# A two-layer retention/latent-attention trunk: one more eviction buffer, a second norm bank, and sums and transfers placed one step ahead

## The chip, the cores and the metric

The kernel runs on one core of a Trainium2 chip. The metric is the device time of one execution in microseconds (us), the median over several runs. A core has a matrix engine (TensorE, PE in the profile), a vector engine (VectorE, DVE), an activation engine (ScalarE, ACT), GpSimd (POOL) and a queue engine (SyncE, SP) that issues most of the transfers. Each engine works through its own list of instructions in order and waits on semaphores for the others. TensorE reads its operands from the on-chip memory (SBUF) and writes sums into PSUM banks of 512 fp32 columns; another engine has to evict a bank before it is used again.

## The reference

One sequence of 512 tokens passes two layers of width 2048; everything is float32. Each layer first normalises its input and modulates it by a conditioning vector c; the branch's output is gated by c too, and added to x.

```python
c_act = jax.nn.silu(c)
for i in range(DEPTH):
    mod = (c_act @ ada_w[i] + ada_b[i])[:, None, :]
    shift, scale, gate = jnp.split(mod, 3, axis=-1)
    h = rmsnorm(x, norm_g[i]) * (1.0 + scale) + shift
    j = i // N_MIXERS
    if i % N_MIXERS == 0:
        y = retention_branch(h, positions, ret_w_in[j], ret_gn_g[j], ret_w_out[j])
    else:
        y = mla_branch(h, positions, mla_w_in[j], ...)
    x = x + gate * y
return rmsnorm(x, final_norm_g)
```

Layer 0 is retention with 8 heads. `h @ w_in` gives q and k (256 columns a head), v and a gate g (512 a head). q and k are rotated by the position, the scores q k^T are multiplied by a decay that falls with the distance of the tokens, and score times v is normalised per head, multiplied by silu(g) and projected back by `w_out`. Layer 1 is latent attention with 16 heads. `h @ w_in` gives two latents of 512 columns (for q and for k, v), a rotary key of 64 columns and a gate of 2048 columns, on which silu is taken; the latents are normalised and projected up to q, k and v, then softmax attention, times the gate, and the output projection.

## The kernel before, in words

Float32 products run as products of two rounded parts: a tile is split into a high part (a cast, on ACT, `split` at L135) and a low part (the difference, on DVE, L136), and each product is three matmuls, high x high, low x high and high x low (L161 to L163, L809 to L811, L1390). Nearly every weight tile therefore passes SP (load), ACT (cast) and DVE (difference) before TensorE can use it. Some products save matmuls by a seven-product scheme (`seven_steps`): it needs sums of the four quarter blocks of the activations (`form_sums`, L447) and combined weights.

The work is a list of steps. A step holds the matmuls of a few weight tiles (a step of a gate block is 24 matmuls of 128x512), and a list "beside" of loads, forming work (ACT, DVE) and extra products that are issued with it. The steps' loads and splits are issued ahead of their products by a fixed number of steps. What a step carries beside is written out by hand; a layer that records the instructions orders those of a step on each engine, and its pools give buffers in rotation, so that a tile waits for the last reader of the one whose buffer it gets.

Three regions matter here, in order of time.

*Retention (about 900 to 1440 us).* `retention(h, ...)` (L1161 on) makes a head out of 14 pieces, and `place` puts piece i beside step first + i. The heads lie at `n_p + 16*(h//2) + 4*(h%2)`: two heads overlap, and four such pairs follow each other. The first pair stands beside the last projection steps, the other three beside the output projection of earlier heads (`o1_product`, L1390, with weights o_r loaded at L1376 and split into o_whi and o_wlo) and beside the modulation sums of the layers to come (`mod`, loaded at L1087 on SP, two buffers, summed on DVE at L1092). The pieces that load are `load_qk(0)` and `load_qk(1)` (two transfers of 256 KB each, tile name qk_r, from DRAM where the projection put q and k; four buffers "ld"), `load_decay` (256 KB, one buffer "dec"), `load_v` (four transfers) and `load_gates` (four). All are on SP's queue with the weight and modulation loads. `rope(n, j)` (DVE, L1156 to L1158, then a split) rotates them, `scores` and `values` multiply on TensorE, `decay_scores` (L1206) applies the decay.

*The front of layer 1 (about 1440 to 1472 us).* The last retention output, the sum of squares, the factors of the norm and the first products of layer 1 overlap, with the tokens in two halves of 256. `norm_sums`, `norm_factors` and `norm_spread` (L1484 to L1494) turn a half's sums of squares into a row of factors that is spread over all partitions by four small matmuls (x_r, L1138) into a PSUM bank `norm2["r"]`, its left columns for half 0, its right for half 1. `h2_pair` (L1499) multiplies x by the factors out of that bank (h2f, DVE, L1505), adds the shift on ACT (the high part, L1512) and forms the low part on DVE (L1517). `ga_half` (L1642) are the products of gate block 0 by a half.

*Gate blocks 0 and 1 (about 1472 to 1550 us) and the latents (from 1550 us).* `g2_steps(gi)` (L1627) makes the eight steps of a gate block: four PSUM banks of 512 columns. At the end `evac` takes silu of each bank on ACT (sgs, L1630) into a buffer of the rotation "sg" (three buffers) and GpSimd stores it to DRAM (sg_d, L1632). `ga` is block 0 and `g1` block 1, `ga[7]` and `g1[7]` their last steps. Beside eight of these steps stands `form_sums` (L1731), which forms the sums for the latents' seven products: two additions (L450), four on half tiles (L452 to L455), then casts and differences; the products themselves (xc, sc, zc, yc, L809 to L811) follow block 1. Beside the last step of block 0 and the first of block 1 the rotary key (kr) is formed on ACT and DVE.

Of the kernel before, what the change touches and what calls it, by code (L numbers as in the profile page):

```python
# [49 lines left out]
def hybrid_trunk_kernel(  # L50
# [44 lines left out]
    def big(name, dt=F32R):  # L95
        return base.tile([P, 2, T], dt, tag="big", bufs=16, name=name)
# [7 lines left out]
    def tmp(name, shape=(P, T)):  # L104
        return base.tile(list(shape), F32, tag="tmp", bufs=6, name=name)
# [4 lines left out]
    def aux(name):  # L110
        return psum.tile([P, T], F32, tag="aux", bufs=4, name=name)
# [41 lines left out]
    def rows(w, u, n, c0, cn):  # L153
        return w[u * n * P : (u + 1) * n * P, c0 : c0 + cn].rearrange("(k p) n -> p k n", p=P)
# [46 lines left out]
    def w_block(w, ki, b):  # L201
        return w[0][:, ki, b * P : (b + 1) * P], w[1][:, ki, b * P : (b + 1) * P]
# [4 lines left out]
    def act_row(t):  # L207
        return t[:, 0, :], t[:, 1, :]
# [13 lines left out]
    a_col = [base.tile([P, KD], F32, name=f"a_col{i}") for i in range(2)]  # L222
# [224 lines left out]
    def form_sums(u, acts, sums, staged, more, late=False, apart=False):  # L447
        e, o = (tmp(f"h_{2 * u + i}_f") for i in range(2))
        for f, kt in ((e, 2 * u), (o, 2 * u + 1)):
            DVE.tensor_add(f, acts[kt][:, 0, :].bitcast(F32), acts[kt][:, 1, :].bitcast(F32))  # L450
        f = staged(f"sums_{u}_f")
        DVE.tensor_add(f[0][:, 0, :], e[:, H:], o[:, H:])  # L452
        DVE.tensor_sub(f[0][:, 1, :], f[0][:, 0, :], e[:, :H])
        DVE.tensor_sub(f[1][:, 0, :], e[:, :H], e[:, H:])
        DVE.tensor_sub(f[1][:, 1, :], o[:, :H], f[0][:, 1, :])  # L455

        def part():
            for i in range(2):
                s = sums[2 * u + i] = sums_tile(u + 8 * i if apart else 2 * u + i, more)
                split(f[i], s[:, :, 0, :], s[:, :, 1, :])  # L460

        if late:
            return part
        part()
# [78 lines left out]
    for t in range(NT):  # L543
        queued(square, t)
        queued(silu, t)
        if t == 0:
            queued(
                lambda: DVE.scalar_tensor_tensor(
                    out=bias1, in0=bias_c[0][:, KD:], scalar=1.0, in1=norm_c[0], op0=ALU.add, op1=ALU.mult
# [191 lines left out]
    def plain_steps(nu, kn, parts, cn, name, take, n, lhs, rhs, evac, seeded=False, **kw):  # L741

        banks = {}

        def step(u):
            w = {}

            def load():
                w["raw"] = base.tile([P, kn, cn], F32, tag="raw", bufs=3, name=f"{name}_{u}_r")
                for dst, src in parts(u):  # L750
                    nc.sync.dma_start(dst(w["raw"]), src)

            def prepare():
                w["hl"] = [
                    base.tile([P, kn, cn], F32R, tag=tag, bufs=3, name=f"{name}_{u}_{tag[1]}") for tag in ("whi", "wlo")
                ]
                split(w["raw"], *w["hl"])

            def multiply():
                if u == 0:  # L760
                    for b in range(n):
                        banks[b] = take(f"{name}_{b}")
                order = [(ki, b) for ki in range(kn) for b in range(n)]
                if u in (0, nu - 1):
                    order = [(ki, b) for b in range(n) for ki in range(kn)]
                for ki, b in order:
                    last = u == nu - 1 and ki == kn - 1
                    kt = u * kn + ki
                    mm3(banks[b], lhs(w["hl"], ki, kt, b), rhs(w["hl"], ki, kt, b), kt == 0, last, seeded)

            def follow():
                if u == nu - 1:
                    for b in range(n):
                        evac(b, banks[b])

            res = Step(load, prepare, multiply, follow, **{k: v(u) for k, v in kw.items()})
            res.w, res.banks = w, banks
            return res

        return [step(u) for u in range(nu)]  # L780
# [354 lines left out]
    def spread(ps, diag, n0, n):  # L1135

        for t in range(n):
            PE.matmul(ps[:, (n0 + t) * P : (n0 + t + 1) * P], ones, diag[:, t * P : (t + 1) * P], start=True, stop=True)  # L1138
# [14 lines left out]
    def rope_half(b1, b2, second, dst, name):  # L1153
        cos, sin = rotary
        t1, t2 = (tmp(f"{name}_t{i}") for i in range(2))
        DVE.tensor_mul(t1, b1, sin if second else cos)  # L1156
        DVE.tensor_mul(t2, b2, cos if second else sin)
        (DVE.tensor_add if second else DVE.tensor_sub)(t1, t1, t2)  # L1158
        split(t1, dst[:, 0, :], dst[:, 1, :])

    def retention(h, own, own2=None):  # L1161


        raws, sg, qk, v, s_hl, aside, ys, yn = {}, [], [], [], [], {}, [], []

        def fetch(key, tag, src_d, r0):
            raws[key] = l1_tile(tag, 4, f"{key}_{h}_r")
            nc.sync.dma_start(raws[key], src_d[r0 : r0 + P, :])

        def load_qk(n):  # L1170
            for j in range(2):
                fetch(f"qk{n}{j}", "ld", qk_d, (4 * h + 2 * n + j) * P)
# [14 lines left out]
        def rope(n, j):  # L1187
            dst = (own2 or own)(f"qk_{h}_{n}_{j}p")
            rope_half(raws[f"qk{n}0"], raws[f"qk{n}1"], j == 1, dst, f"rope_{h}_{n}_{j}")
            qk.append(dst)  # L1190
# [70 lines left out]
        def form_input():  # L1261
# [18 lines left out]
        return [  # L1280
            {"load": lambda: load_qk(0)},
            {"form": lambda: rope(0, 0)},
            {"form": lambda: rope(0, 1)},
            {"load": lambda: load_qk(1)},
            {"form": lambda: rope(1, 0)},
            {"form": lambda: rope(1, 1)},
            {"multiply": scores},
            {"load": load_decay},
            {"load": load_v, "form": decay_scores},
            {"load": load_gates, "form": split_v, "multiply": values},  # L1290
            {"form": group_norm},
# [25 lines left out]
    n_p = len(steps)  # L1317
    steps += block
    heads = [retention(0, k4), retention(1, k4, odd)]


    x1 = []
# [109 lines left out]
    for n in range(3):  # L1432
        block = []
        cols = range(4) if n % 2 == 0 else range(3, -1, -1)
# [35 lines left out]
    for u in range(4):  # L1470
        step = Step()
# [10 lines left out]
    norm2 = {}  # L1482
# [7 lines left out]
        norm2["diag"] = token_factors(norm2["s"], 2 * half, 2, f"x1_{half}")  # L1490

    def norm_spread(half):
        if half == 0:
            norm2["r"] = aux("x1_r")  # L1494
        spread(norm2["r"], norm2["diag"], 2 * half, 2)

    h2 = [None] * KD

    def h2_pair(u, half):  # L1499

        cols = slice(half * H, (half + 1) * H)
        sides = []
        for kt in (2 * u, 2 * u + 1):
            t = tmp(f"h2f_{half}_{kt}")[:, :H]
            DVE.scalar_tensor_tensor(  # L1505
                out=t, in0=x1[u][:, kt % 2, cols], scalar=a_col[1][:, kt : kt + 1], in1=norm2["r"][:, cols],
                op0=ALU.mult, op1=ALU.mult,
            )
            if h2[kt] is None:
                h2[kt] = big(f"h2_{kt}")  # L1510
            hi, lo = (h2[kt][:, a, cols] for a in range(2))
            ACT.activation(hi, t, AF.Identity, bias=b_col[1][:, kt : kt + 1])  # L1512
            sides.append((kt, t, hi, lo))

        def lows():
            for kt, t, hi, lo in sides:
                DVE.scalar_tensor_tensor(  # L1517
                    out=lo, in0=t, scalar=b_col[1][:, kt : kt + 1], in1=hi.bitcast(F32), op0=ALU.add, op1=ALU.subtract
                )

        return lows

    def h2_pairs(*which):

        late = None
        for u, half in which:
            lows = h2_pair(u, half)
            if late is not None:
                late()
            late = lows  # L1530
        late()
# [45 lines left out]
    for i, (multiply, follow) in enumerate(  # L1577
# [5 lines left out]
        step = Step(multiply=multiply, follow=follow)  # L1583
# [40 lines left out]
    def l2_tile(tag, bufs, name, shape=(P, T), dt=F32):  # L1624
        return pools["l2"].tile(list(shape), dt, tag=tag, bufs=bufs, name=name)

    def g2_steps(gi, **kw):  # L1627
        def evac(b, ps):
            sgs = l2_tile("sg", 3, f"sgs_{gi}_{b}")
            ACT.activation(sgs, ps, AF.Silu)  # L1630
            r0 = (gi * 4 + b) * P
            POOL.dma_start(sg2_d[r0 : r0 + P, :], sgs)  # L1632

        return plain_steps(
            8, 2, lambda u: [(whole, rows(w_mla_in, u, 2, 1088 + gi * 512, 512))], 512, f"g2_{gi}", acc, 4,
            lambda w, ki, kt, b: w_block(w, ki, b), lambda w, ki, kt, b: act_row(h2[kt]), evac, **kw,
        )


    ga = g2_steps(0, seeded=True)  # L1640
# [79 lines left out]
    g1 = g2_steps(1)  # L1720
# [7 lines left out]
    def more2(shape, name):  # L1728
        return l2_tile("pt", 4, name, shape, F32R)

    for u, step in enumerate((ga[5], ga[7], g1[0], g1[2], g1[3], g1[5], g1[6], g1[7])):  # L1731
        step.beside["form"].append(lambda u=u: form_sums(u, h2, sums2, staged2, more2, apart=True))

    latent = {}
# [741 lines left out]
```

## Time and profile before

| | |
|---|---|
| median of three runs | 2164.12 us (2163.43 to 2165.03) |
| the profiled execution: its time | 2161.27 us |
| its span, first to last instruction | 2159.4 us |
| mean granted TensorE clock | 0.999 |
| TensorE matmul busy | 2131.3 us, 99% |
| VectorE / ScalarE / GpSimd busy | 1676.7 us, 78% / 1056.4 us, 49% / 106.5 us, 5% |
| TensorE waiting for others, 17 groups | about 19 us in all |

In a row of the timeline stand the start, the length, the engine, the line, the operation with its output and input, and how many were joined (x3); in brackets the idle time of the engine just before it and what ended that. A row of waits reads "engine line waited for: us in total, times, longest". DMA rows give the size of one transfer and the median time from issue to landing. Consecutive matmuls overlap: each has a length of 0.39 us (512 columns), but they start 0.227 us apart.

### The profile page before, as it was taken

How to read it: one execution, taken by the hardware profiler on the slowest of the kernel's cores; microseconds unless marked ns; L12 is line 12 of the kernel's file. 1: busy time of each engine (PE TensorE's matmuls, PEld its weight loads, DVE VectorE, ACT ScalarE, POOL GpSimd, SP SyncE). 2: the span in 40 equal slices, each digit the busy share in tenths (PEclk: the TensorE clock that was granted, in tenths of full speed). 3: DMA queues.
4: the chain of work that ended last, by engine and by line, in shares of the span. 5: the costliest groups of instructions: out<-in, count | busy, mean ns of one | idle time of the engine just before them, and what ended most of it. 6: DMA issues, size and time to landing. Idle time of an engine off the chain costs nothing.

```text
span 2159.4 us, 30016 instructions
## 1 busy us (share of the span) xinstructions
PE 2131.3 (99%) x11100; PEld 1824.7 (84%) x11100; DVE 1676.7 (78%) x2481; ACT 1056.4 (49%) x1604; POOL 106.5 (5%) x178
## 2 busy tenths in 40 slices
PE   8999999999999999999999999999999999999998
PEld 5788898988889888888888888898789999888887
DVE  7998788888878789666777777667877788886755
ACT  5674444444444444434444534344446565664434
POOL 1010000000000000000000000010000000000000
PEclk9999999999999999999999999999999999999999
DMA  9975686877777768755646557553456644346733
GB/s 382 404 276 192 221 278 225 270 243 254 255 258 258 232 230 286 249 197 173 227 164 229 201 190 259 166 176 108 148 194 200 190 136 141 119 138 216 245 110 136
DMA packets 229782, 462.96 MB, mean 214 GB/s; under 512 B 20817, under 2 KB 84337, under 8 KB 225793
## 3 DMA queue, kind: packets, MB, share of 16 engines
q1 hardware_dynamic: 217424, 421.85, 58.8%
q0 software_dynamic: 11920, 38.91, 4.6%
q8 instruction: 87, 1.43, 0.3%
q14 instruction: 61, 0.50, 0.1%
q10 hardware_dynamic: 290, 0.27, 0.0%
HBM read 417.96 MB, written 43.00 MB: 213 GB/s over the span
## 4 chain that ended last, share of the span: by engine, by line
PE 82%; issue 6%; DVE 5%; DMA 4%; ACT 2%; POOL 1%; SPq 0%; POOLq 0%; DVEq 0%; ACTq 0%
PE o L1390 11%; PE o L2312 4%; PE y L810 2%; PE y L811 2%; PE s L810 2%; PE y L809 2%; PE s L811 2%; PE x L811 2%; PE x L810 2%; PE s L809 2%; PE x L809 2%; PE x_qk L908 2%; PE y_qk L908 2%; PE s_qk L908 2%; PE qk L161 2%
## 5 line engine op out<-in xcount | busy, mean ns | idle before, releaser
L1390 PE MATMUL o<-o_h,o_wlo 128*128 128x512 f32 (+1 forms) x496 | 191.6, 386 | 1.5 <-DVE o_wlo L136 1.5
L1390 PE MATMUL o<-o_h,o_whi 128*128 128x512 f32 (+1 forms) x496 | 192.3, 388 | 0.0
L1390 PE MATMUL o<-o_l,o_whi 128*128 128x512 f32 (+1 forms) x496 | 191.3, 386 | 0.0
L1390 PEld LDWEIGHTS o<-o_h,o_wlo 128*128 128x128 f32 x496 | 93.2, 188 | 20.8 <-DVE o_wlo L136 2.1
L136 DVE TENSOR_TENSOR o_wlo<-o_r,o_whi 128x1024 fp32r<-128x1024 f32 x61 | 74.5, 1223 | 45.3 <-ACT o_whi L135 45.3
L1390 PEld LDWEIGHTS o<-o_h,o_whi 128*128 128x128 f32 x496 | 93.2, 188 | 18.5 <-ACT o_whi L135 0.4
L1390 PEld LDWEIGHTS o<-o_l,o_whi 128*128 128x128 f32 x496 | 93.2, 188 | 18.3
L356 DVE SCALAR_TENSOR_TENSOR aw<-aw,c_all 128x2048 f32<-128x2048 f32 (+1 forms) x35 | 73.2, 2104 | 2.6 <-DMA aw<-in_ada_t_dram 2.6
L161 PE MATMUL qk<-hT,qk_h 128*128 128x512 f32 x192 | 74.9, 390 | 0.0
L135 ACT CAST o_whi<-o_r 128x1024 fp32r<-128x1024 f32 x61 | 63.5, 1052 | 22.9 <-PE o L1390 17.6
L162 PE MATMUL qk<-hT,qk_h 128*128 128x512 f32 x192 | 74.7, 389 | 0.0
L163 PE MATMUL qk<-hT,qk_l 128*128 128x512 f32 x192 | 73.4, 389 | 0.0
L1092 DVE SCALAR_TENSOR_TENSOR mod<-mod,c_odd 128x1024 f32<-128x1024 f32 x48 | 58.1, 1221 | 19.7 <-DMA mod<-in_ada_t_dram 19.7
L136 DVE TENSOR_TENSOR o_w_lo<-o_w_raw,o_w_hi 128x1024 fp32r<-128x1024 f32 x32 | 39.0, 1221 | 32.2 <-ACT o_w_hi L135 32.2
L1092 DVE SCALAR_TENSOR_TENSOR mod<-mod,c_bm 128x1024 f32<-128x1024 f32 x48 | 58.5, 1219 | 0.0
L2312 PE MATMUL o<-o_h,o_w_hi 128*128 128x512 f32 (+1 forms) x160 | 55.6, 348 | 0.0
L2312 PE MATMUL o<-o_h,o_w_lo 128*128 128x512 f32 (+1 forms) x160 | 55.5, 347 | 0.0
L2312 PE MATMUL o<-o_l,o_w_hi 128*128 128x512 f32 (+1 forms) x160 | 55.5, 347 | 0.0
L1245 ACT ACTIVATE yn<-y,nmr,gn_r 128x512 f32<-128x512 f32 x32 | 22.3, 777 | 62.0 <-DVE nmr L1239 62.0
L135 ACT CAST o_w_hi<-o_w_raw 128x1024 fp32r<-128x1024 f32 x32 | 33.5, 1050 | 35.9 <-PE o L2312 32.1
L135 ACT CAST o_h<-o_in 128x1024 fp32r<-128x1024 f32 x24 | 25.2, 1052 | 50.9 <-PE o L162 46.9
L161 PE MATMUL o<-o_h,o_w_hi 128*128 128x512 f32 x128 | 50.1, 391 | 0.0
(1607 smaller groups left out, 6901.8 us busy)
## 6 DMA issues: line engine op xcount, KB each, us to landing
mod<-in_ada_t_dram SPq DMA_DIRECT2D x96, 512.0 KB, 5.7
o_r<-in_ret_w_out_dram SPq DMA_DIRECT2D x64, 512.0 KB, 5.5
aw<-in_ada_t_dram SPq DMA_DIRECT2D x30, 1024.0 KB, 9.3
mod_gate<-in_ada_t_dram SPq DMA_DIRECT2D x32, 512.0 KB, 4.7
o_w_raw<-in_mla_w_out_dram SPq DMA_DIRECT2D x32, 512.0 KB, 4.0
qk_r<-in_ret_w_in_dram SPq DMA_DIRECT2D x48, 256.0 KB, 3.2
qk_r<-qk_d SPq DMA_DIRECT2D x32, 256.0 KB, 6.5
v_r<-v_d SPq DMA_DIRECT2D x32, 256.0 KB, 6.4
```

The lines of the kernel that those rows point to most:

```text
L135: ACT.copy(hi, src)
L136: DVE.tensor_sub(lo, src, hi.bitcast(F32))
L161: PE.matmul(o, lhs[0], rhs[0], start=first and not seeded, stop=False, skip_group_check=seeded)
L162: PE.matmul(o, lhs[0], rhs[1], start=False, stop=False, skip_group_check=seeded)
L163: return PE.matmul(o, lhs[1], rhs[0], start=False, stop=last, skip_group_check=seeded)
L809: PE.matmul(banks[b], a[0], w[0], start=first, stop=False, skip_group_check=True)
L810: PE.matmul(banks[b], a[0], w[1], start=False, stop=False, skip_group_check=True)
L811: PE.matmul(banks[b], a[1], w[0], start=False, stop=True, skip_group_check=True)
L908: PE.matmul(o, w[wp][:, i, b * P : (b + 1) * P], a[ap], start=first and i + b + k == 0, stop=k == 2, skip_group_check=True,)
L1092: DVE.scalar_tensor_tensor(out=aw, in0=aw, scalar=1.0, in1=silu_c[j], op0=ALU.mult, op1=ALU.mult, accum_out=mc[:, j, b : b + 1],)
L1390: PE.matmul(o, w[i][:, ki, c0 + b * P : c0 + (b + 1) * P], a[j], start=first and i + j == 0, stop=last and i == 1, skip_group_check=True,)
L2312: PE.matmul(banks2[b][:, cols], w[0][i][:, 0, b * P : (b + 1) * P], o2_moving(w, u, cols)[j], start=u + i + j == 0, stop=u == KD - 1 and i ...
```

## The change

Four edits; no instruction is added or taken away.

- `evac` of a gate block takes the fourth of its four buffers from the pool "tmp" (six buffers) and only the first three from the rotation "sg".
- Each half of the norm's factors has a PSUM bank of its own (`norm2["r", half]`), rather than half of a common one.
- In the list of a retention head's pieces, `load_qk(1)` moves from piece 3 to piece 2 (beside `rope(0, 1)`) and `load_decay` from piece 7 to piece 6 (beside `scores`); empty pieces keep the others where they were.
- Five of the eight `form_sums` move one step ahead: those that stood beside g1[2], g1[3], g1[5], g1[6] and g1[7] stand beside g1[1], g1[2], g1[4], g1[5] and g1[6].

```diff
-            {"form": lambda: rope(0, 1)},
-            {"load": lambda: load_qk(1)},
+            {"load": lambda: load_qk(1), "form": lambda: rope(0, 1)},
+            {},
             {"form": lambda: rope(1, 0)},
             {"form": lambda: rope(1, 1)},
-            {"multiply": scores},
-            {"load": load_decay},
+            {"load": load_decay, "multiply": scores},
+            {},
...
     def norm_spread(half):
-        if half == 0:
-            norm2["r"] = aux("x1_r")
-        spread(norm2["r"], norm2["diag"], 2 * half, 2)
+        norm2["r", half] = aux(f"x1_r{half}")
+        spread(norm2["r", half], norm2["diag"], 2 * half, 2)
...
-                out=t, in0=x1[u][:, kt % 2, cols], scalar=a_col[1][:, kt : kt + 1], in1=norm2["r"][:, cols],
+                out=t, in0=x1[u][:, kt % 2, cols], scalar=a_col[1][:, kt : kt + 1], in1=norm2["r", half][:, cols],
...
-            sgs = l2_tile("sg", 3, f"sgs_{gi}_{b}")
+            sgs = l2_tile("sg", 3, f"sgs_{gi}_{b}") if b < 3 else tmp(f"sgs_{gi}_{b}")
...
-    for u, step in enumerate((ga[5], ga[7], g1[0], g1[2], g1[3], g1[5], g1[6], g1[7])):
+    for u, step in enumerate((ga[5], ga[7], g1[0], g1[1], g1[2], g1[4], g1[5], g1[6])):
```

In the order of instructions that results, SP's queue changes in the retention region (the moved loads stand ahead of the modulation and output-weight loads that they stood behind), DVE and ACT change in gate block 1, and TensorE's order changes in the front, where the spread of the second half no longer stands behind the same products, and at the start of the latents.

## The prediction

> **What bounds the kernel now.** I read the busy table first, then the clock, then what ended the idle time of the busiest engine, and then that engine's own timeline at each place where it paused.
>
> ```profile
> core 0: 2159.4 us, clock 0.999
> ...
> PE 2131.3 (99%) x11100; PEld 1824.7 (84%) x11100; DVE 1676.7 (78%) x2481; ACT 1056.4 (49%) x1604; POOL 106.5 (5%) x178
> ...
> PE o L1390 <- DVE o_wlo L136: 1.5, 1, 1.5
> ...
> PE sc L809 <- ACT sgs L1630: 1.4, 1, 1.4
> ...
> PE x_r L1138 <- DVE h2f L1505: 1.1, 1, 1.1
> ```
>
> TensorE (PE) is busy 99% of the span at a clock of 0.999, so only 28.1 us are idle at all, and much of that is at the start. The change adds and removes no arithmetic, so it can move the time only through these pauses. The waits named are "line <- releaser: us in total, times, longest". All three lie where the change works. A row's wait is less than the whole pause, since the engine also loses a little in getting going again, so I take each pause from the timeline: the distance of two starts less the usual distance of such matmuls (0.23 us for 512 columns, 0.12 for 256).
>
> **Part 1: the fourth eviction buffer and the sums one step ahead.** They meet in the same places and are costed together. The first place is the end of gate block 0, the second the end of gate block 1.
>
> ```profile
> 1508.56 0.60 ACT L1630 ACTIVATE sgs<-g 128x512 f32<-128x512 f32 x1 [1.78 <-DMA sg_d<-sgs]
> ...
> 1517.07 0.39 PE L163 MATMUL g<-h,g_l 128*128 128x512 f32 x1
> ...
> 1517.75 0.50 PE L161 MATMUL g<-h,g_h 128*128 128x512 f32 x1 [0.28 <-ACT g_h L135]
> 1518.09 0.40 PE L162 MATMUL g<-h,g_h 128*128 128x512 f32 x1
> ...
> 1549.81 1.14 ACT L135 CAST sums<-sums_f 128x512 fp32r<-128x512 f32 x2 [3.62 <-DVE sums_f L453]
> 1550.86 1.56 ACT L1630 ACTIVATE sgs<-g 128x512 f32<-128x512 f32 x3
> ...
> 1551.74 1.60 POOL L1632 DMA_DIRECT2D sg_d<-sgs  x3 [41.75 <-ACT sgs L1630]
> ...
> 1555.94 0.60 ACT L1630 ACTIVATE sgs<-g 128x512 f32<-128x512 f32 x1 [3.52 <-DMA sg_d<-sgs]
> ...
> 1551.01 0.39 PE L811 MATMUL zc<-vgc_00o_h,h 128*128 128x512 f32 x1
> 1551.50 0.50 PE L809 MATMUL xc<-vgc_00e_h,h 128*128 128x512 f32 x1
> ...
> 1554.83 0.39 PE L811 MATMUL yc<-vgc_00o_h,sums 128*128 128x512 f32 x1
> 1556.59 0.50 PE L809 MATMUL sc<-vgc_00e_h,sums 128*128 128x512 f32 x1 [1.38 <-ACT sgs L1630]
> ```
>
> In block 0 the fourth eviction waits 1.78 us for the store of the first one to free its buffer, and everything behind it on ScalarE (ACT) is late: the cast of the next weights, the rotary copies, the casts of the sums. The chain reaches PE as a pause of 0.45 + 0.11 us (1517.75 - 1517.07 - 0.23, and the slow restart 1518.09 - 1517.75 - 0.23). With a buffer of its own the fourth eviction follows the third, ACT is 1.8 us ahead, and both are gone: 0.56 us.
>
> In block 1 the same wait is 3.52 us, because the evictions begin late: ACT stands until 1549.81 for the last pair of sums, which DVE has only then formed. PE runs out of free banks and pauses 1556.59 - 1554.83 - 0.23 = 1.53 us, and 0.11 to restart. A smaller pause ahead of it, 0.26 us (1551.50 - 1551.01 - 0.23) with a restart that I take as 0.11 too, comes from the evictions of the first banks. Without the buffer wait, and with the last sums formed one step (5.44 us) before, ACT can evict each bank when it is full, from about 1548.8, and the fourth is done at about 1551, ahead of the first matmul that wants that bank. Both pauses should go with their restarts: 2.0 us. Cover: ACT is idle 3.62 us there, DVE's work on the next weights moves behind the sums and ends near 1550.1, before PE's 1550.56. The buffer comes from a pool of six that the next long users reach some tens of us later, so its store, under 5 us, holds nobody up.
>
> What the move costs: the sums of tiles 3 and 4 now stand before the low parts of the next weights in steps that had none.
>
> ```profile
> 1520.01 1.29 DVE L450 TENSOR_TENSOR h_f<-h 128x512 f32<-128x512 f32 x2
> ...
> 1524.59 1.23 DVE L136 TENSOR_TENSOR g_l<-g_r,g_h 128x1024 fp32r<-128x1024 f32 x1 [0.18 <-ACT g_h L135]
> 1525.73 1.29 DVE L450 TENSOR_TENSOR h_f<-h 128x512 f32<-128x512 f32 x2
> ```
>
> A step with sums takes DVE 1525.73 - 1520.01 = 5.72 us against the 5.44 that PE takes for a step of 24 matmuls (24 x 0.227), so each loses 0.28. Three of them in a row now open the block. With DVE 1.8 us earlier at its start, the low parts of step 3 end at about 1522.9 and of step 4 at about 1528.6; PE would want them at about 1523.2 and 1528.7. It fits with 0.1 us to spare, so I charge 0.1, between 0 and 0.9 (three steps at 0.28). Sum of part 1: 0.56 + 2.0 - 0.1 = 2.5 us, between 1.7 (0.9 lost) and 2.6.
>
> **Part 2: a bank for each half of the norm's factors.**
>
> ```profile
> 1458.45 0.48 DVE L1130 TENSOR_SCALAR x_diag<-ident,x_r 128x128 f32<-128x128 f32 x2 [0.83 <-POOL x_r L131]
> 1458.85 0.87 DVE L1505 SCALAR_TENSOR_TENSOR h2f<-x,a_col,x_r 128x256 f32<-128x256 f32 x2
> ...
> 1459.36 0.91 ACT L1512 ACTIVATE h<-h2f,b_col 128x256 fp32r<-128x256 f32 x2 [3.07 <-DVE h2f L1505]
> ...
> 1459.90 0.88 DVE L1517 SCALAR_TENSOR_TENSOR h<-h2f,b_col,h 128x256 fp32r<-128x256 f32 x2 [0.18 <-ACT h L1512]
> ...
> 1458.35 0.28 PE L1654 MATMUL g<-h,g_l 128*128 128x256 f32 x1
> 1459.77 0.71 PE L1138 MATMUL x_r<-x_diag,ones 128*128 128x128 f32 x4 [1.15 <-DVE h2f L1505]
> ```
>
> The spread of the second half waits until DVE has read the first half's factors out of the same bank. With its own bank it can run at about 1458.8, behind the diagonals, in 0.5 us. But PE's next matmuls need the new tiles: ACT's first high part is there at about 1459.8 and DVE's low part at 1460.4, whatever the bank. So of the 1.31 us pause only the time of the spread itself, about 0.45, is hidden. What is late next is the pair of tiles at 1459.36 and 1459.90. I take 0.45, between 0 and 1.2.
>
> **Part 3: retention's transfers one step ahead.** The loads of a head's second query-key pair and of its decay move ahead in SP's queue; the arithmetic keeps its place. The head before last (third pair) shows the most:
>
> ```profile
> 1255.60 11.90 SPq L1087 DMA_DIRECT2D mod<-in_ada_t_dram  x2
> ...
> 1268.42 0.88 SPq L1168 DMA_DIRECT2D qk_r<-qk_d  x2
> ...
> 1271.60 1.23 DVE L1092 SCALAR_TENSOR_TENSOR mod<-mod,c_odd 128x1024 f32<-128x1024 f32 x1 [2.17 <-DMA mod<-in_ada_t_dram]
> ...
> 1275.65 0.69 DVE L1156 TENSOR_TENSOR rope_t<-qk_r,cos 128x512 f32<-128x512 f32 x1 [1.67 <-DMA qk_r<-qk_d]
> ...
> 1279.71 0.40 PE L1390 MATMUL o<-o_l,o_whi 128*128 128x512 f32 x1
> 1281.56 0.50 PE L1390 MATMUL o<-o_h,o_wlo 128*128 128x512 f32 x1 [1.46 <-DVE o_wlo L136]
> ...
> qk_r<-qk_d SPq DMA_DIRECT2D x8, 256.0 KB, 7.4
> ```
>
> SP stands 11.9 us at two modulation loads (the second waits for a buffer that DVE still reads), the pair's load is queued behind and goes out at 1268.42, and DVE waits 1.67 us for it. DVE then forms the low part of the output weights late and PE pauses 1281.56 - 1279.71 - 0.23 = 1.62 us. After the change the load goes out before the blocked one, at about 1255.6; with the 7.4 us from issue to landing that the last row gives there, it is in place near 1263, ten us early. The modulation load stays blocked to the same moment, so the 2.17 us wait stays. I take 1.7 with the restarts.
>
> ```profile
> 1160.55 0.69 DVE L1156 TENSOR_TENSOR rope_t<-qk_r,cos 128x512 f32<-128x512 f32 x1 [0.77 <-DMA qk_r<-qk_d]
> ...
> 1184.56 0.69 DVE L1206 TENSOR_TENSOR s_0f<-s,dec 128x512 f32<-128x512 f32 x1 [0.21 <-DMA dec<-const_decay_dram]
> ...
> 1191.36 0.39 PE L1390 MATMUL o<-o_h,o_wlo 128*128 128x512 f32 x1
> 1191.95 1.20 PE L161 MATMUL y<-v,sT 128*128 128x512 f32 x4 [0.21 <-ACT v L135]
> ...
> 974.00 10.44 SPq L751 DMA_DIRECT2D qk_r<-in_ret_w_in_dram  x4
> ...
> 989.79 2.18 ACT L135 CAST v<-v_r 128x512 fp32r<-128x512 f32 x4
> ```
>
> One pair earlier DVE waits 0.77 and 0.21 us for the same two loads, and PE pauses 0.36 us (1191.95 - 1191.36 - 0.23) at the value products, whose casts come behind. I credit 0.4, at most the 0.98 that DVE waited. In the other pairs DVE waits too but PE does not, so nothing. What the moves push back: a mod load waits up to about 1 us more for the next pair's buffers, in a queue that stands 11 us for mod buffers anyway; and in the first pair the load of the values falls behind the first two of the four projection loads at 974.00, so goes out at about 975 to 977; ACT wants it at 989.79, 13 us later, so even a landing as slow as 7.4 us is in time. Part 3: 1.7 + 0.4 = 2.1 us, between 0 and 2.7 (1.7 + 0.98).
>
> The Trainium skill's page "DMA: Bandwidth & Descriptors", in "Anatomy of one DMA — SWDGE (gpsimd) path", gives 2.0 us fixed plus the bytes at 436 GB/s, by estimate 2.6 us for 256 KB; the pair would then have landed at 1271, DVE would not have waited, and part 3 would be worth nothing (sum as in the first rival). The trace disagrees here: DVE did wait until 1275.65.
>
> **Sum.** 2.5 + 0.45 + 2.1 = 5.0 us. The profiled execution had a span of 2159.4 us and a time of 2161.27, 2.85 under the median of the runs, 2164.12. Taken off the profile it gives 2156.3, off the median 2159.1.
>
> **The rivals.** A: the transfers are hidden anyway or DVE only waits for the next thing (the 2.17 us mod wait is just ahead of the 1.67), so part 3 gives nothing: 2164.12 - 2.95 = 2161.2. For it: DVE's longest DMA waits are the mod loads, which aren't moved. Against it: DVE ran without a wait from 1275.65 to the late weights. B: DVE is late with low parts in steps 2 to 4 of gate block 1, a new PE wait on g_l of 0.28 us a step that isn't made up, and the seven-step products then start late and find the first weights not ready; part 1 shrinks to 0.5 and the transfers give half: 2164.12 - 0.5 - 0.45 - 1.05 = 2162.1. For it: the 0.1 us of room. Against: the five later steps with sums show no pause now. C, slower: SP's queue. In each of the six later heads the moved loads stand ahead of a modulation or output-weight load; if those land late enough that PE waits once per head as it does at 1281.56 now (1.46 us), that is 6 x 1.46 = 8.8 us against the 2.95 of parts 1 and 2: 2170.0. It decides from 1.2 us a head on ((2.95 + 4.33) / 6 for slower by 0.2%). For it: DVE waits on mod loads today, 2.17 in the row above. Against: the two loads take SP 0.88 us, and the mod load behind them is blocked for 11.9 us by a buffer, not by the queue.
>
> **How the numbers follow.** About 0.2% (4.33 us) is what a measurement of this kernel can tell from no change. Forecast 0.60, A 0.19, B 0.10, C 0.11. The forecast's own range is 2156.8 to 2160.6 (6.5 is the sum of the upper bounds 2.6 + 1.2 + 2.7, with 0.8 for the spread of the runs' median; 3.5 has part 3 at a third of its size); a twentieth of the whole ends short of 4.33. So faster 0.55, same 0.05 + 0.19 + 0.10 = 0.34, slower 0.11. The range for 8 in 10 takes in A and B and leaves out C and the upper end of the gains: 2156.8 to 2163.0.
>
> **What would show it.** Part 1: no ACT wait on sg_d at L1629, no PE wait of sc on sgs, evictions of block 1 starting before 1549; a g_l wait on PE would speak for B. Part 2: x_r of the second half without a wait on h2f, and the pause there about 0.9. Part 3: DVE's waits on qk_r and dec at the third and second pair gone, no PE wait on o_wlo; if PE waits as long for a mod-delayed weight, A or C. I am wrong if the pauses come back a few matmuls later under another name, since every engine then only waited for the next one.

## The result and the profile after

The changed kernel takes 2158.53 us (median of ten runs, 2156.34 to 2160.19), the kernel before 2163.74 us (ten runs, 2162.74 to 2165.03). The ratio is 0.9974, 95% interval 0.9966 to 0.9982: 0.26% faster, 5.2 us by the medians. The forecast was 2159.1 us.

The page, the row of the core and the waits of TensorE from 900 us to the end, of the kernel after:

```profile
core 0: 2154.7 us, clock 0.999
...
PE 2130.0 (99%) x11100; PEld 1825.1 (85%) x11100; DVE 1675.9 (78%) x2481; ACT 1056.5 (49%) x1604; POOL 106.8 (5%) x178
...
PE s L161 <- ACT yn L1245: 1.0, 4, 0.3
PE g L1654 <- ACT h L1512: 0.4, 1, 0.4
PE o L162 <- DVE o_l L136: 0.3, 1, 0.3
...
PE x_r L1138 <- DVE x_diag L1130: 0.3, 1, 0.3
```

None of the three waits of before (o_wlo 1.5, sgs 1.4, h2f 1.1) is left; in the place of the last stand two small ones, on the diagonals (0.3) and on the first new tile (0.4). The profiled execution after took 2156.47 us with a span of 2154.7, 4.7 less than the 2159.4 of before; some 0.5 us of what the change gives is lost again near 2050 us in that execution, in a place that the change doesn't touch (the o_l row).

TensorE works through the same 11,100 matmuls in both kernels, in the same order but for 37 places within the stages, so the distance between two of them, counted by their place in its list, compares a stage in all traces. In us:

| matmuls of TensorE's list | before | after | difference |
|---|---|---|---|
| first 2000 (start to 421 us) | 420.76 | 420.73 | 0.0 |
| 2001 to 5701 (to about 1161 us) | 740.65 | 740.67 | 0.0 |
| 5701 to 7051 (retention, second to fourth pair) | 282.66 | 280.36 | -2.30 |
| 7051 to 7401 (front of layer 1, most of gate block 0) | 57.82 | 57.46 | -0.36 |
| 7401 to 7801 (gate block 1, first latent products) | 93.92 | 91.13 | -2.79 |
| 7801 to 10481 (to about 2035 us) | 439.18 | 439.38 | +0.20 |
| 10481 to the last one | 115.31 | 115.83 | +0.52 |

The three stages of the change give -5.45 us.

*Part 1, gate blocks, after* (timeline of ACT, GpSimd, DVE and TensorE, and a row of the waits of TensorE's weight loads):

```profile
1502.55 2.06 ACT L1630 ACTIVATE sgs<-g 128x512 f32<-128x512 f32 x4
...
1545.91 2.24 ACT L1630 ACTIVATE sgs<-g 128x512 f32<-128x512 f32 x4
...
1546.79 2.19 POOL L1632 DMA_DIRECT2D sg_d<-sgs  x4 [41.17 <-ACT sgs L1630]
...
1518.90 1.23 DVE L136 TENSOR_TENSOR g_l<-g_r,g_h 128x1024 fp32r<-128x1024 f32 x1 [0.18 <-ACT g_h L135]
...
1524.61 2.36 DVE L136 TENSOR_TENSOR g_l<-g_r,g_h 128x1024 fp32r<-128x1024 f32 x2 [0.18 <-ACT g_h L135]
...
1552.56 0.39 PE L811 MATMUL yc<-vgc_00o_h,sums 128*128 128x512 f32 x1
1552.79 0.39 PE L809 MATMUL xc<-vgc_01e_h,h 128*128 128x512 f32 x1
...
PEld g L163 <- DVE g_l L136: 0.2, 1, 0.2
```

Four evictions now run in one row without a wait, in both blocks. The second set starts at 1545.91, against 1550.86 before (3.2 of the 4.95 us are the shift of everything up to there), and is done before the products that need the banks. The matmul `xc<-vgc_01e_h` starts at 1552.79; before it started at 1558.10. A step with sums does take 5.71 us on DVE (1524.61 - 1518.90), but no matmul starts late there; the only wait on a low part in this block is 0.2 us of one weight load (PEld).

*Part 2, the front, after:*

```profile
1456.04 0.28 PE L1654 MATMUL g<-h,g_l 128*128 128x256 f32 x1
1456.58 0.68 PE L1138 MATMUL x_r<-x_diag,ones 128*128 128x128 f32 x4 [0.26 <-DVE x_diag L1130]
1457.62 0.91 PE L1654 MATMUL g<-h,g_h 128*128 128x256 f32 x5 [0.35 <-ACT h L1512]
...
1457.05 0.91 ACT L1512 ACTIVATE h<-h2f,b_col 128x256 fp32r<-128x256 f32 x2 [3.07 <-DVE h2f L1505]
```

The spread of the second half waits for its diagonals alone, and TensorE then waits for the first new tile that ACT writes from 1457.05 on. Before, the distance from the last matmul ahead to the first behind the spread was 1460.24 - 1458.35 = 1.89 us; now it is 1457.62 - 1456.04 = 1.58.

*Part 3, the third pair, after* (SP, DVE and TensorE):

```profile
1254.64 0.80 SPq L1168 DMA_DIRECT2D qk_r<-qk_d  x2
1255.50 10.92 SPq L1087 DMA_DIRECT2D mod<-in_ada_t_dram  x2
...
1270.46 1.23 DVE L1092 SCALAR_TENSOR_TENSOR mod<-mod,c_odd 128x1024 f32<-128x1024 f32 x1 [2.13 <-DMA mod<-in_ada_t_dram]
...
1272.75 0.68 DVE L1156 TENSOR_TENSOR rope_t<-qk_r,cos 128x512 f32<-128x512 f32 x1
...
1277.21 1.22 DVE L136 TENSOR_TENSOR o_wlo<-o_r,o_whi 128x1024 fp32r<-128x1024 f32 x1
...
1279.17 0.39 PE L1390 MATMUL o<-o_l,o_whi 128*128 128x512 f32 x1
1279.39 0.39 PE L1390 MATMUL o<-o_h,o_wlo 128*128 128x512 f32 x1
```

The load goes out ahead of the blocked modulation load, the rotation starts without a wait, the low part of the weights is formed at 1277.21 rather than 1280.29, and the pause of 1.62 us between the last two rows is gone (0.22 apart). The 2.13 us wait for the modulation load stays, as it did before (2.17). One pair earlier, the first value product starts 0.30 us behind the matmul ahead of it, against 0.59 before.

### The profile page after: what moved, and what is told of

Same layout as the page of the kernel before. It is cut to its first block, busy times and chain, and to the rows that moved or that the text cites. A ratio compares the mean times of both kernels' runs of the same rounds, so it can differ in the third digit from the quotient of the medians.

```text
span 2154.7 us, 30027 instructions
## 1 busy us (share of the span) xinstructions
PE 2130.0 (99%) x11100; PEld 1825.1 (85%) x11100; DVE 1675.9 (78%) x2481; ACT 1056.5 (49%) x1604; POOL 106.8 (5%) x178
## 4 chain that ended last, share of the span: by engine, by line
PE 83%; DVE 6%; DMA 5%; issue 2%; ACT 2%; POOL 1%; SPq 0%; DVEq 0%; POOLq 0%; ACTq 0%
PE o L1390 9%; PE o L2312 4%; PE y L810 2%; PE y L811 2%; PE s L810 2%; PE y L809 2%; PE s L811 2%; PE x L811 2%; PE x L810 2%; PE s L809 2%; PE x L809 2%; PE x_qk L908 2%; PE y_qk L908 2%; PE s_qk L908 2%; PE qk L161 2%
## 5 line engine op out<-in xcount | busy, mean ns | idle before, releaser
L162 PE MATMUL o<-o_l,o_w_hi 128*128 128x512 f32 x128 | 50.1, 391 | 0.3 <-DVE o_l L136 0.3
```

Of the source, the lines that this page charges most:

```text
L162: PE.matmul(o, lhs[0], rhs[1], start=False, stop=False, skip_group_check=seeded)
```

## The experiments

All are built on the kernel before unless it is said that they start from the whole change. Distances of two matmuls are taken as in the table above; "retention", "front" and "gate" are its third, fourth and fifth rows (282.66, 57.82 and 93.92 us in the first trace of the kernel before, from which the differences below are taken).

**Part 1 in two: the buffer alone.**

```diff
-            sgs = l2_tile("sg", 3, f"sgs_{gi}_{b}")
+            sgs = l2_tile("sg", 3, f"sgs_{gi}_{b}") if b < 3 else tmp(f"sgs_{gi}_{b}")
```

> Only the fourth eviction buffer. My theory (the sums of part 1 are additive and both edits are wanted): the two ACT waits on sg_d vanish, the pause of 0.56 us in gate block 1 goes and so does the 1.64 us one at the seven products, since the four evictions then run from 1550.9 to 1552.9, but they still begin late behind the last sums, so the 0.37 us pause at 1551 stays: 2.2 us faster. Rival (the late start of the evictions is what counts, the buffer only block 0): 0.6 us faster, and PE still waits over 1 us on sgs.

Ratio 0.9990 (0.9981 to 0.9999). The gate stage takes 91.49 us, 2.43 less. ACT in that trace:

```profile
1550.83 1.14 ACT L135 CAST sums<-sums_f 128x512 fp32r<-128x512 f32 x2 [3.62 <-DVE sums_f L453]
1551.87 2.05 ACT L1630 ACTIVATE sgs<-g 128x512 f32<-128x512 f32 x4
1553.79 1.07 ACT L838 CAST vgc_01e_h<-vgc_01e_r 128x1024 fp32r<-128x1024 f32 x1
```

The evictions still begin late, behind the last sums, but run through, and no matmul waits for the fourth; the small pause of 0.26 us ahead of xc, which comes from the first banks, stays. The rival, that the late start is what counts, falls.

**Part 1 in two: the sums alone.**

```diff
-    for u, step in enumerate((ga[5], ga[7], g1[0], g1[2], g1[3], g1[5], g1[6], g1[7])):
+    for u, step in enumerate((ga[5], ga[7], g1[0], g1[1], g1[2], g1[4], g1[5], g1[6])):
```

> Only the sums one step ahead. My theory: the 0.56 us pause of block 0's end stays, and since ACT and DVE are 1.8 us later at the start of block 1 than in the whole change, the low parts of steps 3 and 4 come late (5.72 us a step against 5.44), a new PE wait on g_l of 0.5 to 1.3 us; the evictions at block 1's end start near 1549 and the fourth waits some 2 us for a store without holding PE up, so 2.0 us go there. Net 0.7 to 1.5 us faster. Rival (sums ahead cost nothing, and are the whole gain of part 1): 2.0 us faster and no wait on g_l.

Ratio 0.9999 (0.9990 to 1.0008): nothing that the times can tell. In the timeline the gate stage takes 93.08 us, 0.84 less (0.5 to 1.1 less than in the eight traces with neither edit, below). The waits of TensorE's weight loads (PEld), two matmuls of gate block 1, and the last eviction:

```profile
PEld g L161 <- ACT g_h L135: 1.5, 3, 0.7
PEld sc L809 <- ACT sgs L1630: 0.8, 1, 0.8
...
1523.63 0.39 PE L163 MATMUL g<-h,g_l 128*128 128x512 f32 x1
...
1524.00 0.50 PE L161 MATMUL g<-h,g_h 128*128 128x512 f32 x1
...
1554.67 0.60 ACT L1630 ACTIVATE sgs<-g 128x512 f32<-128x512 f32 x1 [2.10 <-DMA sg_d<-sgs]
```

Without the buffer, ACT and DVE enter block 1 late, and the steps with sums (5.7 us against 5.44) then do hold TensorE up: two more waits for weights beside the one that was there before, the first seen at 1524.00, a start 0.37 us after the matmul ahead of it instead of 0.23. From the matmul at 1523.63 to the one 48 places on it takes 11.46 us, against 10.88 before: 0.6 us lost. The waits are on the high part (ACT's cast stands behind the casts of the sums) rather than on the low part, as I had put it. The fourth eviction still waits, 2.10 us, and TensorE with it, though I had expected no such wait: the first matmul of sc starts 0.81 us behind the one ahead of it, a pause of 0.58 us. So the two edits are not independent: the buffer gives 2.43, the sums 0.84 alone, both together 2.79, and the sums' move is worth about 0.4 (91.49 against 91.13) once the buffer is there, which is the small pause of 0.26 us and the 0.11 us of its restart. With neither edit this stage takes 93.56 to 94.22 us in eight traces, so a single difference of 0.3 us from those says nothing; with both it takes 91.11 to 91.14 us in four.

**Part 2 alone.**

```diff
-        if half == 0:
-            norm2["r"] = aux("x1_r")
-        spread(norm2["r"], norm2["diag"], 2 * half, 2)
+        norm2["r", half] = aux(f"x1_r{half}")
+        spread(norm2["r", half], norm2["diag"], 2 * half, 2)
```

> Only the second norm bank. My theory: the spread runs behind the diagonals at once and PE then waits for the new tiles; the pause of 1.31 us splits into about 0.4 ahead of the spread and 0.5 behind it: 0.3 to 0.45 us faster, which the times cannot tell from zero but the timeline can. Rival (the whole 1.15 us wait is worth its time): 1.2 us faster and no pause behind the spread.

Ratio 0.9996 (0.9988 to 1.0005), which the times can't tell from zero. The front takes 57.47 us, 0.35 less:

```profile
1459.43 0.28 PE L1654 MATMUL g<-h,g_l 128*128 128x256 f32 x1
1459.98 0.68 PE L1138 MATMUL x_r<-x_diag,ones 128*128 128x128 f32 x4 [0.27 <-DVE x_diag L1130]
1461.01 0.74 PE L1654 MATMUL g<-h,g_h 128*128 128x256 f32 x4 [0.35 <-ACT h L1512]
```

The pause splits in two, as expected. The 1.15 us wait was not worth its time: behind it stood the new tiles, which leave 0.35 us of it to gain. The Trainium skill's page "PSUM — Partial Sum Buffer", in "PSUM bank collisions raise a hardware error", has the program guard PSUM by bank and quadrant, or more simply by bank, and not by address. The trace agrees: with one bank the spread waits 1.15 us for the reader of other columns, with two it does not wait for that reader at all.

**Part 3 alone.**

```diff
-            {"form": lambda: rope(0, 1)},
-            {"load": lambda: load_qk(1)},
+            {"load": lambda: load_qk(1), "form": lambda: rope(0, 1)},
+            {},
...
-            {"multiply": scores},
-            {"load": load_decay},
+            {"load": load_decay, "multiply": scores},
+            {},
```

> Only the transfers one step ahead. My theory: DVE's waits on qk_r and dec in the second and third pair vanish, PE's wait on o_wlo vanishes, 2.1 to 2.3 us faster, and the rest of the trace stays as it was. Rival (transfers hidden anyway, so that the next wait takes their place): no more than 0.4 us faster, with DVE waiting longer on mod.

Ratio 0.9993 (0.9984 to 1.0002). Retention takes 280.36 us, 2.30 less. The two rows where the pause was, and DVE's waits for transfers from 1130 to 1290 us:

```profile
1279.44 0.39 PE L1390 MATMUL o<-o_l,o_whi 128*128 128x512 f32 x1
1279.67 0.39 PE L1390 MATMUL o<-o_h,o_wlo 128*128 128x512 f32 x1
...
DVE mod L1092 <- DMA mod<-in_ada_t_dram: 11.8, 7, 2.1
DVE rope_t L1156 <- DMA qk_r<-qk_d: 0.2, 1, 0.2
```

DVE does not wait longer on mod (11.8 us here, 12.4 in the same window before). The rival falls.

**Part 3 in two: the query-key load alone, the decay alone.** Each is the half of the diff above that its name says.

> Of part 3 only the second query-key load one step ahead. My theory: this is the part that counts; the o_wlo pause of 1.62 us in the third pair goes, and so does the one near 1166 that some runs show behind the same load in the second pair: 1.7 to 2.3 us faster in the timeline, DVE no longer waits on qk_r in those pairs, and only the wait of 0.2 us on dec stays. Rival (SP's queue as a whole is freed, the decay's move counts as much): about half, 1.1 us.

> Of part 3 only the decay's load one step ahead. My theory: DVE's 0.2 us wait on dec goes and nothing else; at most 0.2 us faster in the timeline, the o_wlo pause stays. Rival as above: about 1.1 us.

Ratios 0.9995 (0.9986 to 1.0003) and 0.9996 (0.9988 to 1.0005). Retention takes 280.80 us with the query-key load moved, 1.86 less, as expected; DVE's wait of 0.2 us on dec, which I had expected to stay, is gone too. But it takes 280.64 us with the decay moved, 2.02 less, where I expected 0.2 at most. The pause at the third pair is gone there too, although the query-key load stands where it stood: it goes out as late as before, lands sooner, and DVE finds it in place. Second traces of the kernel before and of the decay's move tell whether that was chance.

> The kernel before, unchanged, looked at a second time, to see which pauses a second execution repeats. If the pause ahead of the late o_wlo in the third pair belongs to the order of the transfers, the load of the second query-key pair lands more than 7 us after its issue again and PE pauses 1.0 to 1.6 us there; the pauses near 1166 and 2040 to 2050, seen in some traces only, may be there or not.

> Only the decay's load one step ahead, a second look. In the first look the query-key load, itself not moved, landed in 5.8 us rather than the 7.1 to 7.4 of four kernels with the old order, and the o_wlo pause was gone. If the decay's move does that, it lands in under 6 us again and the pause stays away; if it was chance, it lands in over 7 us and the pause of 1.0 to 1.6 us is back.

The time from issue to landing of that pair's load, first in the kernel before (two traces), then with the decay moved (two traces):

```profile
DMA to landing us min/median/max: 7.2/7.3/7.4
...
DMA to landing us min/median/max: 6.6/6.7/6.7
...
DMA to landing us min/median/max: 5.7/5.8/5.8
...
DMA to landing us min/median/max: 5.6/5.7/5.8
```

It repeats: 5.6 to 5.8 us with the decay moved, 6.6 to 7.4 with the old order (the second trace of before shows 6.7, not the over 7 that I expected), and the pause stays away in one (retention 280.64 and 280.86) and comes in the other (282.66 and 282.31). In the throughput row of the trace the old order shows a dip just behind the issue of the load, to between 49 and 123 GB/s in a quarter of a microsecond in all six traces that have it, and the two of the decay's move show 148 at the least. The loads beside it are slower too: the two modulation loads around it land in a median of 6.1 to 7.0 us in the old order and in 5.9 with the decay moved, the two weight loads in 7.7 to 8.7 and in 6.8. One explanation is that the decay's buffer, taken earlier, changes where buffers lie in the on-chip memory. The next kernel takes the buffer earlier and leaves its load in place:

```diff
+        def take_decay():
+            aside["dec"] = l1_tile("dec", 1, f"dec_{h}")
+
         def load_decay():
-            aside["dec"] = l1_tile("dec", 1, f"dec_{h}")
             nc.sync.dma_start(aside["dec"], decay[h])
...
-            {"multiply": scores},
+            {"load": take_decay, "multiply": scores},
             {"load": load_decay},
```

> The kernel before, with the buffer of the decay taken one piece earlier but its load issued where it was: every engine's instructions stand in the order of before, only the on-chip memory's allocation sequence differs. If the quicker landing of the query-key load with the decay's move came from where buffers lie, it lands in under 6 us and the o_wlo pause is gone; if it came from the order of the transfers, it lands in 6.6 us or more and PE pauses 1.0 to 1.6 us as before.

Ratio 0.9996 (0.9986 to 1.0006), retention 282.22 us. The load lands late again and DVE waits for it:

```profile
qk_r<-qk_d SPq DMA_DIRECT2D x2, 256.0 KB, 6.9
...
1277.34 0.69 DVE L1156 TENSOR_TENSOR rope_t<-qk_r,cos 128x512 f32<-128x512 f32 x1 [1.48 <-DMA qk_r<-qk_d]
```

So it is where the decay's load is issued, and not the sequence in which buffers are taken. How this makes a later load land sooner stays open. The traces hold one thing that goes with it, a transfer of instructions on the queue q14:

```profile
q1 hardware_dynamic: 496, 1.21, 50.9%
q14 instruction: 1, 0.01, 0.3%
```

The rows are of the kernel before, from 1265.5 to 1273 us (packets, MB, share). A row of q14 stands in that window in all six traces with the late landing, and in neither of the two with the decay moved. By its start in the trace, this 8 KB packet comes 1.5 to 2.2 us behind the load's issue in the six, inside the dip or about half a microsecond behind it at most; with the decay moved it comes 9.5 and 9.8 us ahead of the load, while SP still stands at the modulation loads. Whether it makes the dip or only comes at the same time, no run here separates.

**The whole change, a second trace.**

> The whole change, a second look: no wait of PE on o_wlo, sgs, h2f or g_h, the two pauses of 0.4 and 0.5 us around the norm's spread, and the same four pauses ahead of the odd heads' scores; only the pauses after 2040 and in the first 100 us may differ.

Retention 280.34, front 57.44, gate 91.14 us: all three within 0.02 us of the first trace. What differs lies where it was expected, at the start (421.19 us for the first 2000 matmuls, 420.73 in the first trace) and at the end (116.13 and 115.83).

**What is late next.** Both start from the whole change. The first moves the scores:

```diff
-            {"load": load_decay, "multiply": scores},
-            {},
+            {"load": load_decay},
+            {"multiply": scores},
```

> The whole change, and a head's score products one piece later (into the empty piece behind the decay's load). If the pause ahead of the odd heads' scores (0.38 to 0.47 us and 0.11 to restart, four times) is a wait for the normalisation to free the banks, as the wait row on yn says, one step's delay hides it: 2.0 us more than the whole change gives. Rival (DVE then waits for the scores and the values come late instead): the same pause turns up ahead of y, no gain or up to 2 us lost.

Ratio to the kernel before 0.9972 (0.9962 to 0.9983), against 0.9974 for the change alone: the times do not tell them apart. The distances do: from the 2001st matmul to the 7051st it takes 1018.73 us, against 1021.03 in the change's first trace, 2.30 less, where 2.0 was expected. The four waits on yn are gone from the trace, and one on the weights has come back:

```profile
PE o L1390 <- DVE o_wlo L136: 0.5, 1, 0.5
PE g L1654 <- ACT h L1512: 0.4, 1, 0.4
PE x_r L1138 <- DVE x_diag L1130: 0.2, 1, 0.2
```

The second moves the values too, and interleaves the front:

```diff
-            {"load": load_decay, "multiply": scores},
-            {},
-            {"load": load_v, "form": decay_scores},
-            {"load": load_gates, "form": split_v, "multiply": values},
+            {"load": load_decay},
+            {"load": load_v, "multiply": scores},
+            {"form": lambda: (decay_scores(), split_v())},
+            {"load": load_gates, "multiply": values},
...
-        queued(norm_factors, 1)
-        queued(h2_pairs, (2, 0))
+        root = queued(token_root, norm2["s"], 2, 2, "x1_1")
+        lows = queued(h2_pair, 2, 0)
+        norm2["diag"] = queued(token_diag, root, 2, "x1_1")
+        queued(lows)
```

(`token_root` and `token_diag` are the two halves of `token_factors`.)

> The whole change, the scores one piece later, the values' load and split one piece ahead (beside the decay), and in the norm's front the first new tiles formed while POOL takes the root, ahead of the diagonals. By the timeline of the whole change: 2.0 us from the scores, 1.0 us from the two pauses ahead of and in y (0.53 each), 0.5 us from the pause behind the spread: 3.5 us more than the whole change. Rival (the moved DVE work makes weights late, as it did with the sums): a new PE wait on o_wlo or s, and less than 2 us.

Median 2155.52 us, ratio 0.9964 (0.9952 to 0.9977), the fastest here, though its interval overlaps that of the change alone. In its trace (span 2150.2 us) the first matmul behind the spread starts at 1454.13, against 1457.62 in the change's trace: 3.49 us earlier, the expected 3.5. (The first 2000 matmuls take 420.73 us in both traces.)

```profile
1453.17 0.28 PE L1661 MATMUL g<-h,g_l 128*128 128x256 f32 x1
1453.69 0.68 PE L1145 MATMUL x_r<-x_diag,ones 128*128 128x128 f32 x4 [0.24 <-DVE x_diag L1137]
1454.13 0.60 PE L1661 MATMUL g<-h,g_h 128*128 128x256 f32 x3
...
PE o L1397 <- DVE o_wlo L136: 0.4, 1, 0.4
```

The pause behind the spread is gone; a wait of 0.4 us on o_wlo is what the moved DVE work costs.

## Why the prediction was right

*The sum.* Forecast 5.0 us off the median, measured 5.2, and 5.45 in the three stages of the profile. No rival came. That the parts agree so closely is in part built in, since the forecast read its pauses off the same trace of the kernel before that the stages are compared with. Against the mean of all traces without the edit concerned, the parts give 2.7, 0.4 and 2.2 us, 5.3 in all, so the forecast holds there too.

*Part 1, 2.5 forecast, 2.79 measured.* All the named pauses went (0.56, 1.64, 0.37). The bound was set too tight: 2.6 at most left out a slow start of about 0.1 at 1559.1, and the 0.1 charged for late low parts was not paid. The step "each loses 0.28" was right as a mechanism: it does not show with 1.8 us of head start, and it does when the buffer is taken away, though on the high part. That the stage without the edits varies by 0.7 us makes an excess of 0.2 over the bound a small matter.

*Part 2, 0.45 forecast, 0.36 measured.* The step was right, down to the pair of tiles that is late next; the spread's own time, which I took as fully hidden, is hidden but for the wait on the diagonals.

*Part 3, 2.1 forecast, 2.30 measured, for partly the right reason.* The third pair's pause went as worked out: load at 1254.64, no wait, no pause. It was worth 1.9 us rather than 1.7 (1.63, a restart of 0.11 and two slow starts ahead of it, 0.2 together), and the second pair's 0.3 rather than 0.4. The landing of 2.6 us that the prediction set against this load was no estimate for a load issued by SP; the last section says why. What failed is the step that gave the decay's move next to nothing, on the ground that DVE's wait on it is 0.21 us. Alone it takes the whole pause away, by making another load land sooner. In the sum this cost nothing, since the query-key load's move removes the same pause; the two halves do not add up (1.86 and 2.02, together 2.30).

*What I had not seen* is that the kernel before varies in this stage. Retention takes 281.54 to 283.64 us in the six traces with the old transfer order (before, its second trace, the buffer, the sums, the bank, and the buffer sequence), and 280.34 to 280.36 in the three with the whole of part 3. The forecast took one execution for the size of the pause (1.62 us); in other traces of the old order it is smaller, and another pause on o_wlo appears near 1167 us behind the second pair's load. Part 3 takes both, so its worth against the mean of the six, 282.54, is 2.2 us, and between 1.2 and 3.3 in single executions.

*Rivals.* A (the transfers give nothing) fell with the transfers alone. The mechanism of B (late weights in gate block 1) exists, and is what the sums alone show; the buffer keeps it away. C (SP's queue makes other loads late) fell: no trace with the whole of part 3 and no further change has a new wait of a matmul on weights in retention, and DVE's waits on mod in retention are no longer than before.

## What to carry to other kernels

When the busiest engine is at 99%, list its few pauses, follow each to the queue where the late thing stood, and take the time that the next late thing leaves, not the length of the wait: the three parts of this kernel's gain could be worked out to 0.1 to 0.3 us each that way. Two edits that aim at the same pause do not add, and one may only be safe because of the other, so cost them together and test them apart. Where a pause comes from a transfer's landing, take its size from more than one execution.

## What the runs showed of the hardware

An unchanged 256 KB load, issued at the same place in SP's queue behind the same neighbours, landed in 5.6 to 5.8 us (two traces) or in 6.6 to 7.4 us (six), depending on where another load of this stage was placed; the cause is not shown. The Trainium skill's page "DMA: Bandwidth & Descriptors", in "Anatomy of one DMA — SWDGE (gpsimd) path", gives 2.0 us fixed and the bytes at 436 GB/s for transfers that GpSimd issues, by estimate 2.6 us for 256 KB. The trace agrees for those: the eight stores of 256 KB by GpSimd (sg_d) landed in a median of 2.7 us in the kernel before (2.3 to 4.3). The loads here, with which the prediction compared the figure, are issued by SP beside weight and modulation loads, and none came near it. And executions differ in places that no edit touches: the stage from the 10481st matmul to the last took 115.2 to 117.7 us over the twelve traces of this document that stand ahead of "what is late next", with a wait of TensorE on o_l that is absent in the first trace of before, 0.3 us in the trace of after and 1.8 us with the second bank alone:

```profile
PE o L162 <- DVE o_l L136: 1.8, 3, 0.8
```

That is why the parts, none of which is over 2.8 us, are told apart here by the distances between matmuls and not by the whole time.
